# Bias rows in float32r, loads and sums tied behind other instructions, branch outputs in several DRAM tensors, and a last stage that begins by channel halves

## The chip, the cores and the metric

One Trainium2 chip, one core. The metric is the device time of one execution in microseconds (us), lower is better. The kernel before takes 1904.2 us, the median of 3 runs (1903.38 to 1905.14).

## What is computed

One step of a hybrid decoder layer: 2048 new tokens of one prompt and 8 sequences of 8 new tokens with caches, 2112 token rows in all, model width 1024, all float32. Two branches stand side by side, sliding-window attention with a learned sink and a bias by distance, and gated linear attention (GLA, 4 heads, a running state). Their outputs are projected, gated by channel, added, projected again and normalized.

```python
z = jnp.einsum('btd,dn->btn', x, w_in)
q, k, v, g_att, gq, gk, gv, g_gla, g_lr, r_att, r_gla = jnp.split(z, SPLIT_POINTS, axis=-1)
o_att = swa_prompt(...)        # s = q k / 8 + rel_bias(rel_table, dist); window of 128; softmax with a sink
new_k, new_v = ...             # samples: the cache's rows shifted by 8, then the 8 new rows
o_gla, S = gla(...)            # 4 heads, state 128 x 256 for each
h_att = jnp.einsum('bta,ad->btd', o_att * jax.nn.silu(g_att), w_pa)
h_gla = jnp.einsum('btv,vd->btd', o_gla * jax.nn.silu(g_gla), w_pg)
merged = jax.nn.sigmoid(r_att) * h_att + jax.nn.sigmoid(r_gla) * h_gla
y = jnp.einsum('btd,de->bte', merged, w_o)
x = layer_norm(DN_ALPHA * x + y, ln_g, ln_b)
```

## The kernel before

**Products.** A float32 product is made of three float32r products: each operand is split into a high part (ACT copies it, L113) and a low part (DVE, sometimes POOL, subtracts the high part, L114), and TensorE adds hi·hi, hi·lo and lo·hi in PSUM. `split` is this pair. PSUM has three banks `pd` and five banks `pa`. DVE and ACT evict the banks.

**Four stages.**
1. *Attention*, to about 365 us: six chunks of 384, 384, 384, 384, 256 and 320 tokens. For each chunk, projections k, v, four q, a narrow gl, and four gates ga, each of 8 × 3 products (`proj`, L180 to L182), whose weights come one block of 512 KB at a time (`wload`, L126). Small pieces of work, such as attention scores, wait in a list `side`: `at(d, fn)` puts one d places ahead, and `tick()`, called behind each projection, runs the first place. In chunk 0, `setup1` to `setup3` make the bias rows in this way: 8 products of 32 rows (`rb` against the one-hot `oneh`, L285) go by way of `brow` to a DRAM tensor `bs_d` and are read back shifted. At the last chunk's keys, `win` (L329 on) takes the last window of the chunk before on POOL. The shifted caches are copied straight to the outputs `o_ks` and `o_vs` by two DMAs (L418, L419).
2. *GLA*, to about 1090 us: four heads, each over the six chunks. `gla_store` writes each head's gated output to `ug_d`. `combine_x` loads two blocks of tokens, makes four sums on POOL and stores them (L839) for the stage that follows; 24 of its calls are placed here.
3. *Merge*, 1096 to 1687 us: four passes, with the weights `w_pa`, `w_ra`, `w_rg`, `w_pg`. Each does a two-by-two block product in seven products instead of eight, in the order 1, 2, 7, 6, 5, 3, 4, and each of the seven over three pairs of 352-token blocks: 84 units, numbered n, of four groups (`p`). `raw_x` loads a unit's tokens, `make_x` splits them, `raw_w` and `prep_w` do the like for weights, `partners` loads what an earlier pass left (`cs`), and `combine` evicts the bank and adds it into `a` and `fin` (L1025 to L1039). The last pass ends in `merge_sink`, which stores the merged rows to `mg_d` (L1065). Two kinds of side work are written into the loop over units: the last six `combine_x` calls, whose source is `ug_d`, at every third unit from n = 42, and `wo_load` (L1103) for the first four of eight blocks of `w_o`, at n = 64, 68, 72, 76.
4. *Last stage*, to the end: eight blocks of merged tokens are loaded and split, the other four `w_o` blocks, `lng` and `lnb` are loaded, and for each tile of 128 token rows (17 of them) both halves of 512 channels are projected (`proj_t`, 24 products each, L193 to L195; `proj_s` for the last, narrow tile). DVE adds the scaled input `xr` into `z` and gathers statistics, normalizes, and `o_y` is stored.

**Order of the work.** TensorE keeps the order of the program by hand (`manual_schedule`). The order in which every other engine, and each DMA queue, issues its instructions is fixed when the program is built, by a planner that follows the order of the program as a priority but hoists what is ready, within a pool of tiles, far ahead. A DMA is issued by an engine's queue (SP for `nc.sync`, POOL for `nc.gpsimd`), in that queue's order, and an instruction that waits holds what is behind it. Tiles of one tag are a ring of `bufs` buffers. So the sums and `w_o` loads that the program places at certain units are issued in the trace near 1203 to 1318 us, ahead of their places, and the cache copies of the last chunk at 8.44 us.

Of the kernel before, what the change touches and what calls it, by code (L numbers as in the profile page):

```python
# [21 lines left out]
P = 128  # L22
D = 1024
# [28 lines left out]
def kernel(ctx, tc, io):  # L52
# [28 lines left out]
    ua_d = dram.tile([P, 4, NT], F32, name="ua_d")  # L81
    ug_d = dram.tile([P, 8, NT], F32, name="ug_d")
    mg_d = dram.tile([P, 8, NT], F32, name="mg_d")
    ha_d = dram.tile([P, 8, NT], F32, name="ha_d")
# [27 lines left out]
    def split(dst_h, dst_l, src, eng=nc.vector):  # L112
        nc.scalar.copy(dst_h, src)  # L113
        eng.tensor_tensor(dst_l, src, dst_h.bitcast(F32), ALU.subtract)  # L114

    wseq = [0, 10]
    wready = deque()

    def wload(n=1):
        for _ in range(n):  # L120
            i = wseq[0]
            if i >= wseq[1]:
                return
            wseq[0] += 1
            st = sb.tile([P, D], F32, tag="wst", name="wst", bufs=2)
            nc.sync.dma_start(st, io["wt"][i])  # L126
# [139 lines left out]
    def setup1():  # L266

        oneh, wneg = unit(name="oneh"), unit(name="wneg")
        rtab = small([32, NH], "rtab", 1)
        nc.gpsimd.dma_start(oneh[:32, :LB], io["c_onehot"])  # L270
        nc.gpsimd.dma_start(rtab, io["rel"])
        nc.gpsimd.dma_start(wneg[:, :LB], io["c_win"].broadcast_to([P, LB]))
        nc.gpsimd.dma_start(sink, io["sink"].broadcast_to([P, NH]))
        ssel = unit(name="ssel")[:NH, :2 * P].rearrange("h (a p) -> h a p", a=2)
        scol = small([NH, 1], "scol", 1)
        nc.gpsimd.dma_start(ssel, io["c_ssel"])
        nc.gpsimd.dma_start(scol, io["sink"].rearrange("a h -> h a"))

        rb = wtile(name="rb").rearrange("p (h q) -> p h q", h=NH)[:32]
        nc.vector.tensor_copy(rb, rtab.unsqueeze(2).broadcast_to([32, NH, P]))  # L280
        for h in range(0, NH, 2):
            brow = wtile(name="brow")[:, :2 * LB].rearrange("p (h j) -> p h j", h=2)
            for j in range(2):
                bps = pa()
                mm(bps[:, :LB], rb[:, h + j], oneh[:32, :LB], start=True, stop=True)  # L285
# [28 lines left out]
    def att_keys(A, ps, T):  # L314
# [13 lines left out]
        if A["kprev"] is not None:  # L328
            kp, Tq = A["kprev"]  # L329
            win = wtile(F32R, "win").rearrange("p (a k) -> p a k", a=4)  # L330
            for i in range(4):
                nc.gpsimd.tensor_copy(win[:, i, :W], kp[i][:, Tq - W:Tq])
                nc.gpsimd.tensor_copy(win[:, i, W:], A["k"][i][:, :W])
            A["win"] = win
# [75 lines left out]
    def samp_prep(A, Tp):  # L410
# [6 lines left out]
        A["kc"], A["vc"] = kc, vc  # L417
        nc.gpsimd.dma_start(io["o_ks"][:, 0:W - TS, :], io["ck"][:, TS:W, :])  # L418
        nc.gpsimd.dma_start(io["o_vs"][:, 0:W - TS, :], io["cv"][:, TS:W, :])  # L419

# [111 lines left out]
    for c, (t0, T) in enumerate(CHUNKS):  # L532
# [45 lines left out]
        if c == 0:  # L578
            at(0, setup1)
            at(1, setup2)  # L580
            at(3, setup3)

# [40 lines left out]
        for g in range(G):  # L623
# [3 lines left out]
            if g == 1:  # L627
                xf = fetch_x(io["xT"], *CHUNKS[(c + 1) % len(CHUNKS)])
            if g == G - 2:
# [133 lines left out]
    def gla_store(B):  # L763
        for m in range(2):
            nc.sync.dma_start(ug_d[:, 2 * B["h"] + m, B["t0"]:B["t0"] + B["T"]], B["sg"][m][:, :B["T"]])

# [28 lines left out]
    def samp_b(B, bh):  # L795
# [23 lines left out]
        if bh + 4 == NB:  # L819
# [4 lines left out]
                   [(io["xT"], xc_d, 4, k, s) for s in range(MS) for k in range(4)] +  # L824
                   [(ug_d, uc_d, 4, k, s) for k0 in (0, 2) for s in range(MS) for k in (k0, k0 + 1)])

    def combine_x(new):
        src, dst, kh, k, s = combos.popleft()
        ts = slice(2 * s * MT, 2 * (s + 1) * MT)
        x1, x2 = new("x1")[:, :2 * MT], new("x2")[:, :2 * MT]  # L830
        nc.sync.dma_start(x1, src[:, k, ts])
        nc.sync.dma_start(x2, src[:, kh + k, ts])
        t0, t1 = slice(0, MT), slice(MT, 2 * MT)
# [7 lines left out]
    def chain(B):  # L841
# [10 lines left out]
        if last:  # L852
# [3 lines left out]
            at(nt + 2, lambda B=B: samp_b(B, 4))  # L856
            at(nt + 4, lambda B=B: gla_c(B, "s", NS, B["Tp"]))
            at(nt + 4, lambda B=B: gla_store(B))
        else:
# [102 lines left out]
    class Pass:  # L962
# [31 lines left out]
        def raw_x(self, i, s):  # L994
            x = mtile("xs", 4 * T, 3) if self.kh == 4 else mtile("xc", 2 * T, 5)
            if i in (1, 2, 3):
                k, t = {1: (0, 0), 2: (1, 0), 3: (1, 1)}[i]
                d = self.src[:, k * self.kh:(k + 1) * self.kh, toks(s, t)]
            else:
                d = self.kept[{7: 2, 6: 1, 5: 0, 4: 3}[i]][:, s, :self.kh]  # L1000
            nc.sync.dma_start(x.rearrange("p (k t) -> p k t", t=T), d)
            return x
# [17 lines left out]
        def combine(self, i, p, s, ps, parts):  # L1020
# [11 lines left out]
            elif i == 6:  # L1032
                a, u = acc[p, s, 12], acc[p, s, 21]
                add(a, a, ps, ALU.add)  # L1034
                nc.gpsimd.tensor_tensor(u, u, a, ALU.add)
            elif i == 5:
# [25 lines left out]
    def merge_sink(z, parts, ct, ts):  # L1062
        nc.vector.scalar_tensor_tensor(z, parts[0], 1.0, z, ALU.add, ALU.mult)
        nc.gpsimd.tensor_tensor(z, z, parts[1], ALU.add)
        nc.sync.dma_start(mg_d[:, ct, ts], z)  # L1065

    passes = [Pass(io["w_pa"], 2, ua_d, ac_d, [], store_sink),
              Pass(io["w_ra"], 4, io["xT"], xc_d, [ha_d], gated_sink),
              Pass(io["w_rg"], 4, io["xT"], xc_d, [], gate_sink),
              Pass(io["w_pg"], 4, ug_d, uc_d, [tg_d, ta_d], merge_sink)]  # L1070
    units = [(q, i, s) for q in passes for i in ORDER for s in range(MS)]
# [50 lines left out]
    for n, (q, i, s) in enumerate(units):  # L1122
        if n >= 2 * len(ORDER) * MS and n % 3 == 0 and combos:
            combine_x(lambda t: mtile("xc", 2 * T, 5))
        if n >= 3 * len(ORDER) * MS and n % 4 == 0 and len(wo) < 4:
            wo.append(wo_load(mo, len(wo), 8))
        issue_x(n + 3 if q.kh == 2 else n + 2)
# [21 lines left out]
    sb = phase.enter_context(tc.tile_pool(name="ob", bufs=1, reuse_waits="tile"))  # L1149
    x = load_x(mg_d, 0, TM)  # L1150
    for i in range(len(wo), 8):
# [4 lines left out]
    nc.sync.dma_start(lnb, io["ln_b"].broadcast_to([P, D]))  # L1156
    for t0 in range(0, NT, TM):
        for c0 in range(0, min(TM, NT - t0), P):
            n = min(P, NT - t0 - c0)
            xr = sb.tile([P, D], F32, tag="xr", name="xr", bufs=3)  # L1160
            nc.sync.dma_start(xr[:n], io["x"][t0 + c0:t0 + c0 + n])
            z = sb.tile([P, D], F32, tag="z", name="z", bufs=3)
            lastc = c0 + P >= min(TM, NT - t0)
            if lastc and t0 + TM < NT:
                xn = load_x(mg_d, t0 + TM, min(TM, NT - t0 - TM), samples=(t0 + 2 * TM >= NT))

            end = t0 + c0 + n == NT
            N = 256 if end else 512
            bst = small([P, D // 256, 6], "bst", 2)
            for i in range(D // N):  # L1170
                cs = slice(i * N, (i + 1) * N)
                ps = pd()
                wsl = slice(i * N % 512, i * N % 512 + N)
                if end:
                    rest = small([P, 256], "rest", 2)[:n, :N]
                    proj_s(ps[:, :N], rest, x, c0, wo[i * N // 512], 512, wsl)
                else:
                    proj_t(ps[:, :N], x, c0, n, wo[i * N // 512], 512, wsl)

                nc.vector.scalar_tensor_tensor(z[:n, cs], xr[:n, cs], 2.0 * ALPHA, ps[:n, :N], ALU.mult, ALU.add)  # L1180
                if end:
                    nc.vector.tensor_tensor(z[:n, cs], z[:n, cs], rest, ALU.add)
                nc.vector.bn_stats(bst[:n, i], z[:n, cs])
            mv = small([P, 2], "mv", 2)
            nc.vector.bn_aggr(mv[:n], bst[:n, :D // N].rearrange("p a s -> p (a s)"))
            rs = small([P, 1], "rs", 2)
            nc.gpsimd.tensor_scalar(rs[:n], mv[:n, 1:2], 4.0 * EPS, None, op0=ALU.add)
            nc.gpsimd.tensor_tensor(rs[:n], rs[:n], mhalf[:n], ALU.pow)
            N = 512 if end else D
            for i in range(D // N):  # L1190
# [3 lines left out]
                nc.vector.scalar_tensor_tensor(z[:n, cs], z[:n, cs], rs[:n], lnb[:n, cs], ALU.mult, ALU.add)  # L1194
                nc.sync.dma_start(io["o_y"][t0 + c0:t0 + c0 + n, cs], z[:n, cs])
        x = xn
    phase.close()
# [118 lines left out]
```

## Time and profile before

| | us |
|---|---|
| median of 3 runs | 1904.2 (1903.38 to 1905.14) |
| profiled execution | 1904.76 |
| its span | 1902.9 |
| TensorE busy | 1819.0 (96%) |
| DVE busy | 1243.9 (65%) |
| ACT busy | 847.8 (45%) |
| POOL busy | 518.2 (27%) |
| mean granted clock of TensorE | 0.983 |

The span is what the hardware profiler saw between the first and the last instruction; the profiled execution's own time has about 1.9 us beside it. A line of the timeline gives the start, the length, the engine with its source line and operation, output<-input by the program's names, shapes, and in brackets the idle time of that engine before it with what ended it. "xN" counts instructions that were joined into one line. SPq and POOL lines with DMA_DIRECT2D are the issues of DMAs, not their transfers. The granted clock is a share of TensorE's full speed: 0.50 means that a product takes twice its time. DMA share is the mean busy share of the 16 DMA engines.

### The profile page before, as it was taken

To read this page: it belongs to the slowest core of one execution; us is meant where nothing else is said; L and a number is where in the kernel's file an instruction comes from. 1 tells how busy PE (TensorE), PEld (TensorE's weight loads), DVE (VectorE), ACT (ScalarE), POOL (GpSimd) and SP (SyncE) were. 2 spreads that over 40 slices of the span, in tenths; PEclk is the share of its full clock that TensorE was granted. 3 is DMA by queue.
4 is the path that set the end of the run, shared out by engine and by line. 5 is a ranking of instruction groups with operands and counts; after the bars stand their busy time and mean duration, and the time that the engine had idled before them with its cause. 6 is when DMAs were issued, how large, how long until landed. Compare 5 with 4: busy or idle time off the path is not lost.

```text
span 1902.9 us, 32427 instructions
## 1 busy us (share of the span) xinstructions
PE 1819.0 (96%) x11683; PEld 1725.1 (91%) x11683; DVE 1243.9 (65%) x2552; ACT 847.8 (45%) x1942; POOL 518.2 (27%) x667
## 2 busy tenths in 40 slices
PE   6999999999999999999999799997999999979997
PEld 5988998889999999999999799997999999967886
DVE  4587768755675666557655559648746655956665
ACT  3444546545664664556555453434553543221100
POOL 3310111422134114213321133552322154621121
PEclk8999999999999999999999999998999999989999
DMA  6211012543365236424722289878975866884441
GB/s 223 89 38 41 25 45 86 157 144 115 106 216 179 84 122 227 146 81 147 227 79 61 78 278 309 284 268 297 322 238 169 261 216 214 272 296 168 137 138 60
DMA packets 200929, 316.03 MB, mean 166 GB/s; under 512 B 21720, under 2 KB 162864, under 8 KB 200752
## 3 DMA queue, kind: packets, MB, share of 16 engines
q1 hardware_dynamic: 195520, 307.70, 49.5%
q0 software_dynamic: 5248, 6.26, 1.2%
q8 instruction: 92, 1.51, 0.3%
q14 instruction: 69, 0.57, 0.1%
HBM read 228.72 MB, written 86.14 MB: 165 GB/s over the span
## 4 chain that ended last, share of the span: by engine, by line
PE 77%; DMA 8%; DVE 5%; POOL 4%; ACT 3%; issue 2%; SPq 1%; POOLq 0%; DVEq 0%; ACTq 0%
PE pd L180 9%; PE pd L181 9%; PE pd L182 9%; PE pa L1142 7%; PE pa L1141 7%; PE pa L1143 7%; PE pd L193 6%; PE pd L195 6%; PE pd L194 6%; PE pa L401 2%; DMA wst<-w_o 1%; DMA cs<-tg_d 1%; PE pa L386 1%; PE pa L731 1%; PE pa L732 1%
## 5 line engine op out<-in xcount | busy, mean ns | idle before, releaser
L180 PE MATMUL pd<-x,wh 128*128 128x384 f32 (+2 forms) x1248 | 409.6, 328 | 8.4 <-ACT x L113 5.3
L182 PE MATMUL pd<-x,wl 128*128 128x384 f32 (+2 forms) x1248 | 403.6, 323 | 1.3 <-DVE wl L114 1.3
L181 PE MATMUL pd<-x,wh 128*128 128x384 f32 (+2 forms) x1248 | 403.8, 324 | 0.9 <-DVE x L114 0.9
L1141 PE MATMUL pa<-xh,wh 128*128 128x352 f32 x1176 | 382.7, 325 | 17.7 <-DVE a L1034 9.7
L1142 PE MATMUL pa<-xl,wh 128*128 128x352 f32 x1176 | 380.6, 324 | 7.6 <-DVE xl L114 7.3
L1143 PE MATMUL pa<-xh,wl 128*128 128x352 f32 x1176 | 379.8, 323 | 0.0
L180 PEld LDWEIGHTS pd<-x,wh 128*128 128x128 f32 x1248 | 236.8, 190 | 17.8 <-issue 8.1
L1141 PEld LDWEIGHTS pa<-xh,wh 128*128 128x128 f32 x1176 | 222.2, 189 | 19.6 <-DVE a L1034 10.0
L181 PEld LDWEIGHTS pd<-x,wh 128*128 128x128 f32 x1248 | 236.8, 190 | 2.3 <-DVE x L114 2.1
L182 PEld LDWEIGHTS pd<-x,wl 128*128 128x128 f32 x1248 | 236.3, 189 | 1.9 <-DVE wl L114 1.9
L1142 PEld LDWEIGHTS pa<-xl,wh 128*128 128x128 f32 x1176 | 223.2, 190 | 11.9 <-DVE xl L114 11.8
L1143 PEld LDWEIGHTS pa<-xh,wl 128*128 128x128 f32 x1176 | 221.9, 189 | 0.0
L114 DVE TENSOR_TENSOR xl<-xs,xh 128x1408 fp32r<-128x1408 f32 x63 | 108.0, 1714 | 75.9 <-ACT xh L113 61.8
L113 ACT CAST x<-xst 128x384 fp32r<-128x384 f32 (+3 forms) x164 | 77.9, 485 | 160.2 <-PE pd L194 121.4
L193 PE MATMUL pd<-wh,x 128*128 128x256 f32 x512 | 148.0, 289 | 0.0
L194 PE MATMUL pd<-wh,x 128*128 128x256 f32 x512 | 144.9, 283 | 0.3 <-POOL x L114 0.2
L195 PE MATMUL pd<-wl,x 128*128 128x256 f32 x512 | 144.6, 282 | 0.0
L113 ACT CAST xh<-xs 128x1408 fp32r<-128x1408 f32 x63 | 86.4, 1372 | 99.5 <-PE pa L1143 75.4
L723 POOL TENSOR_SCALAR sq<-sq 128x1 f32<-128x1 f32 (+1 forms) x68 | 17.8, 262 | 375.3 <-ACT ring L722 375.3
L193 PE MATMUL pd<-woh,x 128*128 128x512 f32 x256 | 101.8, 398 | 13.2 <-ACT x L113 9.8
L194 PE MATMUL pd<-woh,x 128*128 128x512 f32 x256 | 101.3, 396 | 0.9 <-DVE x L114 0.9
L195 PE MATMUL pd<-wol,x 128*128 128x512 f32 x256 | 101.3, 396 | 0.6 <-DVE wol L114 0.5
(310 smaller groups left out, 3753.1 us busy)
## 6 DMA issues: line engine op xcount, KB each, us to landing
wst<-wt SPq DMA_DIRECT2D x33, 512.0 KB, 3.6
xs<-xc_d SPq DMA_DIRECT2D x24, 704.0 KB, 5.5
u<-xT SPq DMA_DIRECT2D x84, 192.0 KB, 3.9
xst<-xT SPq DMA_DIRECT2D x76, 192.0 KB, 2.7
xs<-xT SPq DMA_DIRECT2D x18, 704.0 KB, 6.1
ws<-w_ra SPq DMA_DIRECT2D x36, 256.0 KB, 4.7
ws<-w_rg SPq DMA_DIRECT2D x36, 256.0 KB, 5.1
ws<-w_pg SPq DMA_DIRECT2D x36, 256.0 KB, 3.9
```

What stands on the lines that cost most here:

```text
L113: nc.scalar.copy(dst_h, src)
L114: eng.tensor_tensor(dst_l, src, dst_h.bitcast(F32), ALU.subtract)
L180: mm(ps, hi[:, s], xh[:, :T], start=(k == 0), stop=False)
L181: mm(ps, hi[:, s], xl[:, :T], start=False, stop=False)
L182: mm(ps, lo[:, s], xh[:, :T], start=False, stop=(k == n - 1))
L193: mm(ps, xh[:, xs], hi, start=(k == 0), stop=False)
L194: mm(ps, xl[:, xs], hi, start=False, stop=False)
L195: mm(ps, xh[:, xs], lo, start=False, stop=(k == KT - 1))
L401: mm(ot[pr, :], vb[:, pr], A["pT", bi, kv][:, hf], start=(hf == h0), stop=(hf == 1))
L1141: mm(ps, wh[:, ks], xh[:, ts], start=(k == 0), stop=False)
L1142: mm(ps, wh[:, ks], xl[:, ts], start=False, stop=False)
L1143: mm(ps, wl[:, ks], xh[:, ts], start=False, stop=(k == q.kh - 1))
```

## The change

- **Start.** `setup1` makes the bias rows with two float32r products (a high and a low part of `rb`, the one-hot in float32r) in place of one in float32, and the three setup pieces run one tick later. The two cache copies are tied behind the last `win` copy, and the activation loads of chunk 1 behind the last weight load that has been written. Such a tie (`issue_after`) puts instructions of the same engine behind the named one in the issue order; it adds no wait on a semaphore.
- **DRAM tensors.** `ug_d` becomes four tensors, one for each head; `mg_d` three, one for each token pair. Loads that cross a boundary become two DMAs. In `raw_x` a block of `ug_d` is two DMAs.
- **GLA.** For heads 0 to 2 the samples' last step and store are put one place later in the list.
- **Merge.** `combine_x` is tied behind the last `raw_x` load (SP) and the last L1035 addition (POOL); `wo_load` behind the last `raw_x` load (SP) and the last high-part copy (ACT).
- **Last stage.** The rows of the loop become a class `Rows`. In the first three tiles the first half of the channels is projected for all three, and then the second half with the norm, tile by tile. `xr` and `z` have four buffers in place of three, the statistics four in place of two, and the `xr` of three tiles are loaded together.

```diff
+        pin["a"] = nc.scalar.copy(dst_h, src)
+            pin["w"] = nc.sync.dma_start(st, io["wt"][i])
...
+        oh = unit(F32R, "oh")[:32, :LB]
+        nc.scalar.copy(oh, oneh[:32, :LB])
+        rbh, rbl = (wtile(F32R, n).rearrange("p (h q) -> p h q", h=NH)[:32] for n in ("rbh", "rbl"))
+        nc.vector.tensor_copy(rbh, rt)
+        nc.vector.tensor_tensor(rbl, rt, rbh.bitcast(F32), ALU.subtract)
...
-                mm(bps[:, :LB], rb[:, h + j], oneh[:32, :LB], start=True, stop=True)
+                mm(bps[:, :LB], rbh[:, h + j], oh, start=True, stop=False)
+                mm(bps[:, :LB], rbl[:, h + j], oh, start=False, stop=True)
...
+        with tc.issue_after(pin["k"].ins):
+            nc.gpsimd.dma_start(io["o_ks"][:, 0:W - TS, :], io["ck"][:, TS:W, :])
+            nc.gpsimd.dma_start(io["o_vs"][:, 0:W - TS, :], io["cv"][:, TS:W, :])
...
-            at(0, setup1)
-            at(1, setup2)
-            at(3, setup3)
+            at(1, setup1)
+            at(2, setup2)
+            at(4, setup3)
...
+                with tc.issue_after(pin["w"].ins) if c == 0 else nullcontext():
+                    xf = fetch_x(io["xT"], *CHUNKS[(c + 1) % len(CHUNKS)])
...
+            o = nt + 4 if B["h"] == GH - 1 else nt + 5
+            at(o, lambda B=B: gla_c(B, "s", NS, B["Tp"]))
+            at(o, lambda B=B: gla_store(B))
...
+            with tc.issue_after(pin["x"].ins), tc.issue_after(pin["p"].ins):
+                combine_x(lambda t: mtile("xc", 2 * T, 5))
...
+            with tc.issue_after(pin["x"].ins), tc.issue_after(pin["a"].ins):
+                wo.append(wo_load(mo, len(wo), 8))
...
+    def load_m(t0, T, samples=False):
+        x = []
+        for k in range(KT):
+            st = xstage()
+            for s in range(t0 // (2 * MT), (t0 + T - 1) // (2 * MT) + 1):
+                a, b = max(t0, 2 * MT * s), min(t0 + T, 2 * MT * (s + 1))
+                nc.sync.dma_start(st[:, a - t0:b - t0], mg_d[s][:, k, a - 2 * MT * s:b - 2 * MT * s])
+            x.append(part((st, T), samples=samples))
+        return x
...
+    for t0 in range(0, NT, TM):
+        T = min(TM, NT - t0)
+        tiles = [Rows(x, t0, c0, T) for c0 in range(0, T, P)]
+        if t0 == 0:
+            for r in tiles:
+                r.product(0)
+        for r in tiles:
+            if r is tiles[-1] and t0 + TM < NT:
+                x = load_m(t0 + TM, min(TM, NT - t0 - TM), samples=(t0 + 2 * TM >= NT))
+            for i in range(1 if t0 == 0 else 0, D // r.N):
+                r.product(i)
+            r.norm()
```

More of the change, by code (lines that the diff above doesn't have):

```diff
@@ L2 @@
 from collections import deque
-from contextlib import ExitStack
+from contextlib import ExitStack, nullcontext
 import numpy as np
@@ L81 @@
     ua_d = dram.tile([P, 4, NT], F32, name="ua_d")
-    ug_d = dram.tile([P, 8, NT], F32, name="ug_d")
-    mg_d = dram.tile([P, 8, NT], F32, name="mg_d")
+    ug_d = [dram.tile([P, 2, NT], F32, name=f"ug{h}_d") for h in range(GH)]
+    mg_d = [dram.tile([P, 8, 2 * MT], F32, name=f"mg{s}_d") for s in range(MS)]
     ha_d = dram.tile([P, 8, NT], F32, name="ha_d")
@@ L824 @@
                    [(io["xT"], xc_d, 4, k, s) for s in range(MS) for k in range(4)] +
-                   [(ug_d, uc_d, 4, k, s) for k0 in (0, 2) for s in range(MS) for k in (k0, k0 + 1)])
+                   [(None, uc_d, 4, k, s) for k0 in (0, 2) for s in range(MS) for k in (k0, k0 + 1)])
     def combine_x(new):
@@ L830, in combine_x @@
         x1, x2 = new("x1")[:, :2 * MT], new("x2")[:, :2 * MT]
-        nc.sync.dma_start(x1, src[:, k, ts])
-        nc.sync.dma_start(x2, src[:, kh + k, ts])
+        for x_, k_ in ((x1, k), (x2, kh + k)):
+            nc.sync.dma_start(x_, ug_d[k_ // 2][:, k_ % 2, ts] if src is None else src[:, k_, ts])
         t0, t1 = slice(0, MT), slice(MT, 2 * MT)
@@ L1034, in combine @@
                 add(a, a, ps, ALU.add)
[L1035 removed]
+                pin["p"] = nc.gpsimd.tensor_tensor(u, u, a, ALU.add)
             elif i == 5:
@@ L1064, in merge_sink @@
         nc.gpsimd.tensor_tensor(z, z, parts[1], ALU.add)
-        nc.sync.dma_start(mg_d[:, ct, ts], z)
+        s = ts.start // (2 * T)
+        nc.sync.dma_start(mg_d[s][:, ct, ts.start - 2 * s * T:ts.stop - 2 * s * T], z)
     passes = [Pass(io["w_pa"], 2, ua_d, ac_d, [], store_sink),
@@ L1069 @@
               Pass(io["w_rg"], 4, io["xT"], xc_d, [], gate_sink),
-              Pass(io["w_pg"], 4, ug_d, uc_d, [tg_d, ta_d], merge_sink)]
+              Pass(io["w_pg"], 4, None, uc_d, [tg_d, ta_d], merge_sink)]
     units = [(q, i, s) for q in passes for i in ORDER for s in range(MS)]
@@ L1156 @@
     nc.sync.dma_start(lnb, io["ln_b"].broadcast_to([P, D]))
[L1157 to L1186, printed above, removed]
@@ new lines, with __init__, product, norm @@
+    class Rows:
+        def __init__(self, x, t0, c0, T):
+            self.x, self.r0, self.c0, self.n = x, t0 + c0, c0, min(P, T - c0)
+            self.end = self.r0 + self.n == NT
+            self.N = 256 if self.end else 512
+            self.xr, self.z = (sb.tile([P, D], F32, tag=n, name=n, bufs=4) for n in ("xr", "z"))
+            nc.sync.dma_start(self.xr[:self.n], io["x"][self.r0:self.r0 + self.n])
+            self.bst = small([P, D // 256, 6], "bst", 4)
+        def product(self, i):
+            n, N, xr, z, end = self.n, self.N, self.xr, self.z, self.end
+            cs = slice(i * N, (i + 1) * N)
+            ps = pd()
+            wsl = slice(i * N % 512, i * N % 512 + N)
+            if end:
+                rest = small([P, 256], "rest", 2)[:n, :N]
+                proj_s(ps[:, :N], rest, self.x, self.c0, wo[i * N // 512], 512, wsl)
+            else:
+                proj_t(ps[:, :N], self.x, self.c0, n, wo[i * N // 512], 512, wsl)
+            nc.vector.scalar_tensor_tensor(z[:n, cs], xr[:n, cs], 2.0 * ALPHA, ps[:n, :N], ALU.mult, ALU.add)
+            if end:
+                nc.vector.tensor_tensor(z[:n, cs], z[:n, cs], rest, ALU.add)
+            nc.vector.bn_stats(self.bst[:n, i], z[:n, cs])
+        def norm(self):
+            n, z = self.n, self.z
+            mv, rs = small([P, 2], "mv", 2), small([P, 1], "rs", 2)
+            nc.vector.bn_aggr(mv[:n], self.bst[:n, :D // self.N].rearrange("p a s -> p (a s)"))
```

35 lines of the change are left out of this document (15 added, 20 removed).

## The prediction

> **What bounds the kernel now.** I read the page first: its span, the busy row and the clock strip.
>
> ```profile
> span 1902.9 us, 32427 instructions
> PE 1819.0 (96%) x11683; PEld 1725.1 (91%) x11683; DVE 1243.9 (65%) x2552; ACT 847.8 (45%) x1942; POOL 518.2 (27%) x667
> PEclk8999999999999999999999999998999999989999
> ```
>
> TensorE is busy for 1819.0 of 1902.9 us, and the clock strip (40 slices, tenths of full speed) dips in three places: the 1st, the 28th and the 36th. The change leaves the float32r products as they are, so it can win only what is left: 83.9 us of idle time, and time in which TensorE is busy but at half clock. Next I read the waits of TensorE, over the span (columns: total us, times, longest) and, in the two rows after them, over the first 31 us alone.
>
> ```profile
> PE pd L193 <- ACT x L113: 9.8, 2, 9.2
> PE pa L1141 <- DVE a L1034: 9.7, 1, 9.7
> PE pa L285 <- DVE rb L280: 5.1, 1, 5.1
> ...
> PE pd L180 <- ACT wh L113: 3.1, 2, 1.9
> PE pd L182 <- DVE wl L114: 1.3, 2, 0.6
> ```
>
> The longest waits stand where the clock dips: the bias rows and first weights (start), one stall in the merge, and the entry of the last stage. Each is now taken from the timeline.
>
> **Start: the copies of the caches.** The change issues both copies (480 KB each) and the early activations of chunk 1 later.
>
> ```profile
> 8.44 0.52 POOL L418 DMA_DIRECT2D o_ks<-ck  x1
> ...
> 11.24 0.33 SPq L126 DMA_DIRECT2D wst<-wt  x1
> 11.61 1.80 SPq L145 DMA_DIRECT2D xst<-xT  x3
> 15.36 16.25 SPq L126 DMA_DIRECT2D wst<-wt  x5
> ...
> 20.32 1.04 ACT L113 CAST wh<-wst 128x1024 fp32r<-128x1024 f32 x1 [5.06 <-DMA wst<-wt]
> 21.41 0.45 PE L180 MATMUL pd<-x,wh 128*128 128x384 f32 x1 [1.94 <-ACT wh L113]
> ```
>
> The copies go out at 8.44 us, ahead of the first weights and beside them; ACT then stands 5.06 us for a weight and TensorE 1.94 us behind it. The waits for weights up to 31 us are 3.1 + 1.3 = 4.4 us. A 480 KB copy reads and writes as much as nearly two weight blocks, so its absence, with that of three activation loads on SP's queue, should bring every early weight in some microseconds sooner. I take 4.0 (bounds 1.5, if the weights are late through their own 16-engine transfer, to 4.7). Where the copies go now, behind the last window copy of chunk 5, nothing waits for them: they write outputs. The later activation loads feed chunk 1 only.
>
> **Start: bias rows.** Rows of TensorE and DVE, then three windows (columns: window, length, busy us and count of PE, PEld, DVE, ACT, POOL, then granted clock, DMA share, GB/s).
>
> ```profile
> 30.03 1.23 DVE L114 TENSOR_TENSOR wl<-wst,wh 128x1024 fp32r<-128x1024 f32 x1 [0.31 <-ACT wh L113]
> 31.18 0.67 DVE L280 COPY rb<-rtab 32x1024 f32<-32x1024 f32 x1
> 31.90 10.60 PE L285 MATMUL pa<-oneh,rb 32*128 32x384 f32 x16 [5.12 <-DVE rb L280]
> 43.08 0.69 PE L180 MATMUL pd<-x,wh 128*128 128x384 f32 x1
> ...
> 30.00:40.00 10.00, 8.10 (x13) 4.41 (x14) 4.62 (x8) 1.05 (x2) 1.12 (x2) 0.55 0.49 176
> 40.00:50.00 10.00, 10.00 (x36) 8.72 (x36) 3.04 (x6) 0.15 (x1) 5.50 (x11) 0.60 0.73 241
> 60.00:70.00 10.00, 10.00 (x60) 9.62 (x58) 5.43 (x7) 3.71 (x6) 4.66 (x12) 1.00 0.64 166
> ```
>
> Before: TensorE stops at 31.90 − 5.12 = 26.78, because `rb` is made behind a weight split on DVE and the setup needs it; 16 fp32 products follow in 10.60 us, and the next projection begins at 43.08, so 16.3 us go by. That projection (24 products) runs at about 0.60 clock: a full-clock step is 10.00/60 = 0.167 us, hence 24 × 0.167 / 0.60 = 6.7. With the value transposes of the next tick, estimated at three steps, 0.5, together 23.5.
>
> After: the setup runs one tick later, so the projection fills the hole at full clock, 24 × 0.167 = 4.0, and the 0.5 of transposes follow. The new operands `rbh`, `rbl` take their place in the ring of weight tiles one weight later, behind the next split: 31.26 + 1.23 + 0.67 + an unseen 32x1024 subtract, estimated at 0.67 to 1.8 between the copy and a 128x1024 split, or about 34.3; TensorE is free at 26.78 + 4.5 = 31.3. It waits about 3.1 (bounds 0, all ready, and 5.12, as now). Then 16 float32r products: not in the trace with 32 rows; bounds are 0.167 full clock (2.7 in all) and the 0.66 of today (10.6). I take 0.33, twice the full-clock row, since clock 0.5 will hold: 5.3, and 0.6 of sink products (43.08 − 42.50). The projection behind them pays the 2.7 of slow clock that the other paid. Sum 4.5 + 3.1 + 5.9 + 2.7 = 16.2 against 23.5, **gain 7.3** (bounds 0, with products of 0.66 and a wait of 5.12, and 15.7, with no wait, 2.7 of products and no slow clock). The one-hot copy on ACT and one more DVE instruction are below 1 us and hidden by the projection; setup2 and setup3, a tick later, feed attention a chunk on.
>
> [...] In the trace 10.6 us of unbroken 32-row products stayed at 0.55 and 0.60, and only full products lifted it, some 5 us after 43.08. [...]
>
> **Merge: the stall at 1283–1304 us.** This is where the ties on sums and output weights act.
>
> ```profile
> 1238.97 0.43 PE L1142 MATMUL pa<-xl,wh 128*128 128x352 f32 x1 [1.24 <-DVE xl L114]
> 1271.77 9.65 SPq L839 DMA_DIRECT2D uc_d<-xc  x7
> 1289.87 1.04 ACT L113 CAST woh<-wst 128x1024 fp32r<-128x1024 f32 x1 [15.44 <-DMA wst<-w_o]
> 1290.95 1.78 DVE L114 TENSOR_TENSOR wol<-wst,woh 128x1024 fp32r<-128x1024 f32 x1 [15.01 <-ACT woh L113]
> 1293.22 0.66 PE L1141 MATMUL pa<-xh,wh 128*128 128x352 f32 x1 [9.68 <-DVE a L1034]
> 1299.61 0.43 PE L1142 MATMUL pa<-xl,wh 128*128 128x352 f32 x1 [2.21 <-DVE xl L114]
> ...
> 1290.00:1295.00 5.00, 1.78 (x6) 1.78 (x7) 4.05 (x5) 4.27 (x5) 4.92 (x4) 0.50 1.00 374
> 1300.00:1305.00 5.00, 5.00 (x24) 5.00 (x23) 4.87 (x11) 3.15 (x5) 0.36 (x1) 0.66 0.91 285
> 1318.00 1.05 ACT L113 CAST woh<-wst 128x1024 fp32r<-128x1024 f32 x1 [0.77 <-DMA wst<-w_o]
> ```
>
> The output weights, written for the last pass, are hoisted far ahead: at 1289.87 ACT has stood 15.44 us for `w_o`, whose load waits on SP's queue behind stores of the sums (`uc_d`, seven issues over 9.65 us), themselves waiting for POOL. DVE stands 15.01 us behind ACT with the evictions of the product banks queued after it, and TensorE runs out of banks: 9.68, then 2.21 for a split made late, and 1.24 at 1238.97 among the same hoisted sums. At half clock (0.50 from 1293.22 to about 1297) some 1.8 us are lost, and in the other window 24 products take 5.00 us, where the row below has 19.29/121 = 0.159 us each: 1.2 more, 3.0 together. With the ties, sums issue unit by unit in the third pass, and `w_o` in the fourth, each behind the last activation load and the last split: gone are 9.68 + 2.21 + 1.24 + 3.0 = 16.1.
>
> What is late next: a tied `w_o` split on ACT waits for its own load while later splits and evictions stand behind it. The nearest row is 1318.00, a wait of 0.77, with no PE idle; four at up to 0.5 each are 2.0 (bounds 0 and 8). The fourth pass also has less room on the DMA engines:
>
> ```profile
> 1660.00:1680.00 20.00, 19.29 (x121) 18.99 (x119) 15.28 (x20) 2.75 (x2) 9.83 (x9) 1.00 1.01 341
> ```
>
> At its end the share is 1.01 and 0.71 us are lost in 20; I take as much again, 0.75, for 4 × 512 KB more in that pass. **Gain 16.1 − 2.75 = 13.4** (bounds 5, half the stall back elsewhere, to 18). The loads of `ug_d` in two pieces cost 9 more issues on SP, hidden by loads two units ahead.
>
> **Entry of the last stage.** First the order of SP's queue, then TensorE.
>
> ```profile
> 1688.31 4.86 SPq L1065 DMA_DIRECT2D mg_d<-a  x4
> 1693.22 1.87 SPq L145 DMA_DIRECT2D xst<-mg_d  x4
> 1696.84 0.80 PE L193 MATMUL pd<-woh,x 128*128 128x512 f32 x1 [9.15 <-ACT x L113]
> 1710.16 0.50 PE L193 MATMUL pd<-woh,x 128*128 128x512 f32 x1 [1.10 <-ACT woh L113]
> 1711.42 0.50 PE L195 MATMUL pd<-wol,x 128*128 128x512 f32 x1 [0.53 <-DVE wol L114]
> 1714.85 0.80 PE L193 MATMUL pd<-woh,x 128*128 128x512 f32 x1 [2.24 <-ACT woh L113]
> ...
> 1714.83 1.23 DVE L114 TENSOR_TENSOR wol<-wst,woh 128x1024 fp32r<-128x1024 f32 x1 [3.47 <-ACT woh L113]
> 1715.00:1720.00 5.00, 4.96 (x11) 3.47 (x12) 4.02 (x7) 1.00 (x2) 0.00 (x0) 0.50 0.56 206
> 1740.00:1760.00 20.00, 20.00 (x90) 16.55 (x89) 12.85 (x18) 2.03 (x4) 3.76 (x4) 1.00 0.48 166
> ```
>
> The second half of the channels needs four weights loaded only now. With three products of the first half ahead, 72 × 20.00/90 = 16 us and a little for the slow first microseconds, TensorE is busy until about 1716.5 from 1696.84; the last weight is ready at 1714.83 + 1.23 = 1716.06. So it is just covered: gone are 1.10 + 0.53 + 2.24, and the half clock of 1714.85 to about 1720.5 (5.6/2 = 2.8). **Gain 6.7** (bounds 3, if loads of `xr` ahead of the weights make these late by 4, and 8). The longer tail of z tiles is covered by a fourth buffer. The 9.15 stays: `mg_d` in three tensors lets the first tokens depend only on their own stores, but those were exact by region already, and the loads stand in SP's order behind the last stores (1688.31, then 1693.22). The straddling loads add 16 issues, spread under products. The samples' step one tick later in three heads falls to the same drain: nothing.
>
> **Sum.** 4.0 + 7.3 + 13.4 + 6.7 = 31.4. The profiled execution took 1904.76 (span 1902.9), which would come to 1873.4; the median of the runs stands 0.6 lower: 1904.2 − 31.4 = **1872.8**.
>
> **Rivals.**
> - *The split tensors free the first loads* (0.15): if SP's order changes so that the first loads pass the last stores, most of the 9.15 and the 1.7 of slow clock behind it go as well, some 10: 1862. Against it stands the queue's order above.
> - *The stall only moves* (0.18): the sums, four in turn for 9 units, still wait on POOL in the third pass and hold its loads, or `w_o` does so in the fourth; the 13.4 are lost and 18.0 stay: 1886. For it: DMA share 1.00 at the stall and 1.01 late in the fourth pass.
> - *Slower* (0.06): each of the four `w_o` loads in the fourth pass stalls ACT as at 1289.87. It decides once ACT stands longer than the five banks last, 5 × 12 × 0.159 = 9.5, as with 15.44. Then 4 × (9.68 + 2.21 + 3.0) = 60 are paid, less 16.1 + 18.0 gained: +26, about 1930. Against it: 1318.00 waited 0.77.
> - *The ties and orders do not move what issues* (0.04): the old order returns, about 1904.
>
> **How the numbers follow.** My own case has 0.57. The range 1855 to 1890 holds it with its bounds, most of the second rival's case and the first's; it leaves out the two dear cases and the ends. A measurement here can tell about 0.2% (3.8 us). Faster 0.90: my case and the first two rivals (0.57 + 0.15 + 0.18); same 0.04, where nothing moves; slower 0.06.
>
> **Right or wrong, in the changed profile.** The cache copies stand near chunk 5, and the waits for weights before 31 us are under 1 us. The bias rows are 16 float32r products near 0.33 us, behind a projection at full clock. No wait of L1034 or of its like over 2 us in the merge; `w_o` splits lie in the fourth pass; the 28th slice keeps clock 9. In the last stage the wait near 9 us remains, and none over 1 us stands before the second half. I am wrong if `w_o` or the sums show ACT or SP waits over 9 us in the passes where they land, if the bias rows wait over 5 us, or if the first load of `mg_d` comes before the last store.

## The result, and the profile after

The changed kernel takes 1880.31 us (median of 4 runs, 1876.45 to 1884.79), the kernel before 1904.67 in the same comparison (1903.38 to 1906.19). The ratio is 0.9873, with a 95% interval of 0.9849 to 0.9896: 24.4 us less, where 31.4 were forecast; the forecast time of 1872.8 was 7.5 us too low, and the range of 1855 to 1890 held the result. The profiled execution of the changed kernel took 1876.45 us, the lowest of the four, 28.3 below the profiled one of before.

The page of the changed kernel:

```profile
span 1874.7 us, 32471 instructions
PE 1812.2 (97%) x11683; PEld 1725.5 (92%) x11683; DVE 1246.1 (66%) x2553; ACT 847.6 (45%) x1943; POOL 517.2 (28%) x667
PEclk8999999999999999999999989999999999989998
```

Of its waits of TensorE (total us, times, longest), those at the places of the change and at the merge's entry:

```profile
PE pd L194 <- ACT x L113: 8.7, 2, 8.4
PE pa L1158 <- ACT wh L113: 6.9, 1, 6.9
PE pa L1159 <- DVE xl L114: 4.8, 5, 1.6
PE pa L290 <- DVE rbh L284: 4.7, 1, 4.7
```

The 9.7 us behind L1034 are gone, and so is the clock's dip in the 28th slice. The wait of the bias rows is still there, 4.7 for 5.1. A dip stands in the 24th slice (1078 to 1125 us), which the change hardly touches: it is the entry of the merge, where TensorE waits 6.9 us for `wh` and the granted clock is 0.53 from 1086 to 1092 us and 0.62 from there to 1098. The kernel before waits 7.2 there and has 0.54 from 1092 to 1098, at the border of two slices, so that its strip does not show it.

The two timelines by stage, in us: the first gate of chunk 0 is evicted at 58.13 (before 65.48), the last gate of the GLA stage at 1076.11 (1079.97), the merge's first product starts at 1091.74 (1095.87), the last stage's at 1676.33 (1696.84), and the span ends at 1874.7 (1902.9). So the lead is 7.4 behind the start, only 3.9 at the end of the GLA stage, 4.1 at the merge, 20.5 at the last stage and 28.2 at the end.

*The start.* The changed kernel's timeline, DVE and TensorE:

```profile
29.38 1.22 DVE L114 TENSOR_TENSOR wl<-wst,wh 128x1024 fp32r<-128x1024 f32 x1 [1.92 <-ACT wh L113]
30.63 0.55 DVE L349 SCALAR_TENSOR_TENSOR qa<-pd,qa 64x384 fp32r<-64x384 f32 x1
31.20 0.56 DVE L350 SCALAR_TENSOR_TENSOR qb<-pd,qb 64x384 fp32r<-64x384 f32 x1
31.79 0.56 DVE L581 COPY vt<-pa 128x384 f32<-128x384 f32 x1
32.38 0.68 DVE L284 CAST rbh<-rtab 32x1024 fp32r<-32x1024 f32 x1
...
33.21 0.66 PE L290 MATMUL pa<-oh,rbh 32*128 32x384 f32 x1 [4.70 <-DVE rbh L284]
40.10 0.69 PE L181 MATMUL pd<-x,wh 128*128 128x384 f32 x1
```

Two of its windows, columns as in the prediction:

```profile
34.00:40.00 6.00, 5.64 (x19) 5.64 (x19) 4.65 (x9) 1.04 (x1) 0.65 (x2) 0.50 0.40 147
40.00:45.00 5.00, 5.00 (x16) 4.99 (x17) 2.63 (x5) 0.00 (x0) 2.80 (x6) 0.50 1.00 281
```

The projection does fill the old hole, but `rbh` is not made beside it. It stands on DVE behind the next weight split (29.38 to 30.60, as the prediction had it) and then behind that projection's own evictions (`qa`, `qb`, `vt`, 1.7 us together), which run only after TensorE is done at 28.51. The 16 products go at 0.32 us as forecast (19 in 6.00 us with the sink products), at a granted clock of 0.50, and the projection behind them begins at 0.50 too.

*The merge.* The changed kernel's timeline, one of the tied sums in the third pass and one of the tied output weights in the fourth:

```profile
1355.81 0.95 POOL L842 TENSOR_TENSOR xc<-xc 128x352 f32<-128x352 f32 x1 [2.54 <-DMA xc<-ug_d]
...
1561.24 0.42 SPq L1120 DMA_DIRECT2D wst<-w_o  x1
1567.56 1.05 ACT L113 CAST woh<-wst 128x1024 fp32r<-128x1024 f32 x1 [8.43 <-DMA wst<-w_o]
```

Both stand where they were tied. ACT waits 8.43 us for `w_o`, much more than the 0.77 I had taken, and still TensorE has no wait over 1.6 us in the merge behind its first product: the banks cover it.

*The last stage.* The changed kernel's timeline, SP's queue and TensorE's first product:

```profile
1668.53 4.53 SPq L1080 DMA_DIRECT2D mg_d<-a  x4
1673.11 1.87 SPq L1174 DMA_DIRECT2D xst<-mg_d  x4
1676.33 0.80 PE L194 MATMUL pd<-woh,x 128*128 128x512 f32 x1 [8.41 <-ACT x L113]
```

Then the split of the last of the four weights that the second half needs, and the window in which the products of the second half begin (the first at 1696.42):

```profile
1693.93 1.23 DVE L114 TENSOR_TENSOR wol<-wst,woh 128x1024 fp32r<-128x1024 f32 x1 [2.80 <-ACT woh L113]
...
1696.33:1702.33 6.00, 6.00 (x29) 4.95 (x28) 3.82 (x8) 0.93 (x2) 0.00 (x0) 1.00 0.65 200
```

The first loads of merged rows stand behind the last stores, as before. The waits for `woh` and `wol` are gone: the last weight is ready at 1695.16, 1.3 us before its first use, and TensorE is busy in every microsecond of 1696 to 1702.

### The profile page after: what moved, and what is told of

Same layout as the page of the kernel before. It is cut to its first block, busy times and chain, and to the rows that moved or that the text cites. A ratio compares the mean times of both kernels' runs of the same rounds, so it can differ in the third digit from the quotient of the medians.

```text
span 1874.7 us, 32471 instructions
## 1 busy us (share of the span) xinstructions
PE 1812.2 (97%) x11683; PEld 1725.5 (92%) x11683; DVE 1246.1 (66%) x2553; ACT 847.6 (45%) x1943; POOL 517.2 (28%) x667
## 4 chain that ended last, share of the span: by engine, by line
PE 80%; DMA 6%; DVE 5%; POOL 3%; ACT 3%; issue 2%; SPq 1%; POOLq 0%; DVEq 0%; ACTq 0%
PE pd L181 9%; PE pd L182 9%; PE pd L183 9%; PE pa L1159 8%; PE pa L1158 8%; PE pa L1160 8%; PE pd L195 6%; PE pd L196 6%; PE pd L194 6%; PE pa L407 2%; PE pa L392 1%; PE pa L739 1%; PE pa L740 1%; PE pa L738 1%; DMA cs<-tg_d 1%
## 5 line engine op out<-in xcount | busy, mean ns | idle before, releaser
L181 PEld LDWEIGHTS pd<-x,wh 128*128 128x128 f32 x1248 | 237.2, 190 | 15.6 <-issue 8.1
L114 DVE TENSOR_TENSOR xl<-xs,xh 128x1408 fp32r<-128x1408 f32 x63 | 111.9, 1776 | 74.5 <-ACT xh L113 55.6
L195 PEld LDWEIGHTS pd<-wh,x 128*128 128x128 f32 x512 | 98.4, 192 | 2.4 <-DVE x L114 2.4
```

The costliest lines, as they stand in the source:

```text
L181: mm(ps, hi[:, s], xh[:, :T], start=(k == 0), stop=False)
L195: mm(ps, xl[:, xs], hi, start=False, stop=False)
```

## The experiments

My theory after the two traces: the parts add, and start, merge and last stage bring 7.4, 15.6 and 7.7 us in the profiled executions (between the merge's first product and the last stage's the lead grows by 16.4; 0.7 of it is the shorter wait at the last stage's entry). What was open: why the first gate's lead was 7.4 and not 11.3, what took 3.5 us of it back before 1080 us, and why the median stands 4 us above the profiled execution. Times below are medians, each beside the kernel before on the same chip, with the ratio's 95% interval.

**The changed kernel again.** No edit.

> The changed kernel unaltered. Its first four runs spread over 8.3 us (1876.45 to 1884.79), the kernel before over 2.8. Theory: the spread comes from the output weights in the fourth pass, where ACT stood 8.43 us for w_o at 1567.56 and the five banks last about 9.5; then a slower profiled run shows TensorE waiting some us behind a w_o split there, and the other stages as in the first profile. Rival: it comes from the start or the GLA stage (clock at half after short idle times, some 1.5 us each); then the fourth pass looks as in the first profile and the loss stands before 1095 us. Both expect 1876 to 1885.

1877.75 against 1905.22, ratio 0.9856 (0.9837 to 0.9876). In its profile (1877.12, not one of the longer executions) the fourth pass has no wait of TensorE over 1.6 us. In the GLA stage the clock held at 1067 us, but fell at another place: the granted clock is 0.57 from 723 to 727 us. And the kernel before, 17 runs here, spread from 1899.08 to 1908.13 by itself. So the spread that I wished to explain belongs to no part of the change: the first theory fell, and of the rival only the clock (below) is shown.

**The start alone.** The diff's part for `setup1`, the ticks, the cache copies and `fetch_x`, on the kernel before.

> The kernel before with the start's part alone: bias rows in float32r, setup one tick later, both cache copies tied late, activation loads of chunk 1 tied. Theory (the parts add, and the start brought 7.4 us by the first gate and 5.4 by the end of the GLA stage): 1897 to 1900, spread under 4 us, TensorE waiting over 4 us for rbh. Rival (the loss of 2.0 us near 319 us and the half clock near 1067 us belong to other parts of the change): 1897 with the full 7.4 kept to 1090 us.

1895.58 against 1905.22, ratio 0.9952 (0.9936 to 0.9967): 9.6 us less, somewhat more than either theory; the spread, 1893.19 to 1902.67, is more than the 4 of the theory. First gate at 57.49, wait for `rbh` 4.17. Its lead of 8.0 there has shrunk to 2.5 where the merge starts (1093.35 for 1095.87): 2.0 are lost near 319 us as in the changed kernel, and the clock falls at 1066 us here too. So these losses are no matter of the other parts, and the rival fell. But this was the longest of six executions, and the other five took 1897.39 or less: the rest of the loss is not the kernel's for certain.

**The merge alone.**

```diff
+            with tc.issue_after(pin["x"].ins), tc.issue_after(pin["p"].ins):
+                combine_x(lambda t: mtile("xc", 2 * T, 5))
...
+            with tc.issue_after(pin["x"].ins), tc.issue_after(pin["a"].ins):
+                wo.append(wo_load(mo, len(wo), 8))
```

> The kernel before with the ties of the sums and of wo_load alone. Theory (this part took 15.6 us out of the merge in the profile, and carries the spread): 1889 to 1897, spread over 4 us, a wait of ACT for w_o of 5 to 12 us in the fourth pass. Rival (the stall moves with time as soon as a transfer is late): 1900 or more. The other rival (spread from elsewhere): 1889 to 1890 with a spread under 3 us.

1889.35, ratio 0.9917 (0.9900 to 0.9935): 15.9 us less, as the profiles had it. The spread was 7.9, and ACT's longest wait for `w_o` in the fourth pass 7.67, both as the theory had them.

**The last stage alone.** `Rows` with `load_x` from one `mg_d`.

> The kernel before with the last stage by channel halves alone (four buffers of xr and z), merged rows in one tensor as before. Theory: the wait for the other four weights goes, 7.7 us, and the entry's wait near 9 us stays: 1896 to 1898, spread under 3 us. Rival (the DRAM split is needed for the entry): the wait of the entry is longer than the 8.4 us of the changed kernel by more than 0.7, and 1897 to 1900.

1902.20, ratio 0.9989 (0.9977 to 1.0002): 3.0 us less, not 7.7, and the interval takes in no change at all; the spread was 11.1. The entry's wait was 8.16. The theory had the right waits and the wrong worth. Compare the first product of the last stage to the end: 200.5 us here, 198.4 in the changed kernel, 206.1 in the profile of before; but the six other kernels of this document whose last stage is that of before have 201.5 to 205.9. The window just behind the wait for the last weight in the kernel before (granted clock: third column from the end):

```profile
1716.84:1722.84 6.00, 6.00 (x20) 4.73 (x19) 4.60 (x7) 1.00 (x2) 1.97 (x2) 0.69 0.41 136
```

And in the kernel with the start alone:

```profile
1717.39:1723.39 6.00, 6.00 (x28) 4.96 (x27) 5.43 (x9) 0.97 (x2) 1.98 (x2) 1.00 0.44 143
```

The same work, 20 products against 28 in 6 us: the profiled execution of before had lost its clock there, and the other had not. What I had counted as the kernel's is partly the execution's. Of the seven profiles with the old last stage, before and the loads alone had 6.8 us of half clock behind those weights, the merge alone and its two parts 3.4, the start alone and the bias rows alone none; TensorE waited 0.3 to 4.1 us for the four weights. Over the seven the stage took 204.3 us in the mean, and over the seven profiles with the new one 199.2 (198.3 to 201.4): about 5 us, between the 3.0 of the times and the 7.7 of the first pair.

**Parts of the start.** First the copies and the loads of chunk 1 alone, then the float32r rows alone, at the old tick.

> The kernel before with the cache copies and the activation loads of chunk 1 tied late, nothing else. Theory (the early weights shared the DMA engines with the copies): the waits for weights up to 31 us fall from 4.4 to about 1.2 us, the first gate of chunk 0 comes 2.5 to 3.5 us earlier than at 65.48, the time 1901 to 1903. Rival (the weights are late through their own transfers): 4 us of waits remain, 1905.

The waits of TensorE before 31 us, in this kernel:

```profile
PE pa L286 <- DVE rb L281: 4.1, 1, 4.1
PE pd L183 <- DVE wl L114: 0.4, 1, 0.4
```

4.4 us of waits for weights became 0.4, and the first gate came at 60.87, 4.6 earlier. The mechanism is shown; the time, 1903.25 against 1904.35, ratio 0.9990 (0.9975 to 1.0005), does not stand clear of no change. The loads of chunk 1 and the cache copies were moved together here; which of them held up the weights was not tried. In chunk 5 a wait appears that the kernel before does not have there:

```profile
321.81 1.07 PE L402 MATMUL pa<-pT,vt 128*64 128x512 f32 x2 [1.13 <-DVE pT L389]
```

The lead falls there from 4.6 to 2.6 us.

> The kernel before with the float32r bias rows alone, the setup at its old tick. Theory (the later tick brought nothing, since the new wait for rbh, 4.0 to 4.7 us behind the evictions of the next projection on DVE, stands for the old one of 4.1 to 5.1): 16 products at 0.32 us after a wait near 5 us, first gate 4.5 to 5.5 us earlier, the time 1899 to 1901, and this with loads_only makes the 9.6 of the start. Rival (the later tick is worth the projection in the hole, 2 to 3 us, as predicted): first gate only 2 to 3 us earlier, 1902 to 1903.

The first of the float32r products in its timeline:

```profile
33.21 0.66 PE L289 MATMUL pa<-oh,rbh 32*128 32x384 f32 x1 [5.32 <-DVE rbh L283]
```

And the window over the products:

```profile
34.00:40.00 6.00, 5.64 (x19) 5.64 (x19) 4.65 (x9) 0.08 (x1) 0.33 (x1) 0.50 0.59 215
```

First gate at 62.99, 2.5 earlier than before's; 1900.31, ratio 0.9973 (0.9960 to 0.9985). The gate's lead is the rival's, the time the theory's. By the gates, 4.6 and 2.5 of the 7.4 to 9.0 (five profiles with the whole start) are these two, and the later tick is left with 0.3 to 1.9 us. But the first gate comes at 64.14 to 67.43 in the five profiles with the old start, so what the tick is worth stays open between the theory's nothing and the rival's 2 to 3.

**Parts of the merge.** The sums' tie alone, and the `w_o` tie alone.

> The kernel before with the ties of combine_x alone; the w_o loads keep their old hoisted places. Theory (w_o was late because it stood behind the stores of the sums on SP): the wait of 9.7 us goes, as w_o no longer stands behind them, 1889 to 1892. Rival (the hoisted w_o loads stall ACT anyway, by DMA share 1.00): a wait over 5 us stays near 1290 us, 1897 to 1901.

1892.48, ratio 0.9933 (0.9916 to 0.9951): 11.9 us less. In this kernel TensorE's waits between 1200 and 1330 us are short, nearly all for splits:

```profile
PE pa L1144 <- DVE xl L114: 2.9, 3, 1.2
PE pa L1143 <- ACT xh L113: 0.6, 1, 0.6
PE pa L1143 <- DVE fin L1029: 0.3, 1, 0.3
```

The `w_o` loads still come early here, but no longer behind the sums' stores, and ACT waits 3.9 us for them at most.

> The kernel before with the ties of wo_load alone; the six sums stay hoisted near 1203 to 1300 us. Theory (the stall needs both: ACT in order behind a late w_o): the 9.7 goes here as well, and a smaller loss of 1 to 4 us stays where SP stands behind the sums, 1890 to 1895. Rival (SP standing behind the sums delays the units' own loads): over 5 us stay near 1290 us, 1897 to 1901.

1898.86, ratio 0.9961 (0.9947 to 0.9976): 5.5 us less. The 7.9 us that stay have another last link. TensorE's wait in this kernel between 1200 and 1330 us:

```profile
PE pa L1143 <- DVE a L1040: 7.9, 1, 7.9
```

And its timeline, SP's queue and DVE:

```profile
1274.77 10.83 SPq L840 DMA_DIRECT2D uc_d<-xc  x7
1300.18 0.64 SPq L1057 DMA_DIRECT2D ta_d<-fin  x1
1306.48 0.52 DVE L1039 TENSOR_TENSOR fin<-a,pa 128x352 f32<-128x352 f32 x1 [8.47 <-DMA ta_d<-fin]
```

SP stands behind the stores of the sums, so the stores of finished rows (`ta_d`) come late, their `fin` buffers are not free, and DVE, with nothing to do with `w_o`, holds the banks. The cause is the hoisted sums on SP's queue; `w_o` was only the first to suffer. The rival was right here.

**The operands one tick earlier.** On the changed kernel, `setup1` in two:

```diff
+        st1["ops"] = oh, rbh, rbl, wneg, ssel, scol
+
+    def setup1b():
+        oh, rbh, rbl, wneg, ssel, scol = st1["ops"]
...
-            at(1, setup1)
+            at(0, setup1)
+            at(1, setup1b)
```

> The changed kernel with setup1 in two: the operands oh, rbh, rbl and the small loads one tick earlier (place 0), the products at place 1 as in the change. Theory (the wait of 4.0 to 4.7 us for rbh is only its place on DVE behind the evictions of the next projection): no wait over 1 us for rbh, first gate 4.5 us or more earlier than 57.2 to 58.1, so 51 to 53; if without the idle time the clock stays full through the 16 rows and the next projection, another 4 to 5. Time 1868 to 1874. Rival (rbh is late because rtab, oneh or a tile comes late): the wait stays over 3 us, 1877 to 1880.

Its timeline, DVE and TensorE:

```profile
27.17 0.68 DVE L284 CAST rbh<-rtab 32x1024 fp32r<-32x1024 f32 x1
31.41 0.56 DVE L585 COPY vt<-pa 128x384 f32<-128x384 f32 x1
...
32.03 0.68 PE L294 MATMUL pa<-oh,rbh 32*128 32x384 f32 x1 [1.40 <-DVE vt L585]
```

And its windows:

```profile
28.00:32.00 4.00, 2.16 (x11) 1.42 (x9) 3.90 (x5) 2.50 (x4) 0.00 (x0) 0.87 0.60 179
32.00:36.00 4.00, 3.97 (x13) 3.87 (x14) 4.00 (x10) 1.04 (x1) 0.00 (x0) 0.50 0.73 270
```

`rbh` is ready at 27.85 and the products begin at 28.24 with no wait; first gate at 53.80, 3.4 to 4.3 earlier than with the change, a little less than the theory's 4.5. After eight products the banks are full, since DVE still has `qa`, `qb` and `vt` ahead of the first `brow`: a wait of 1.40, and the clock falls after all. The products before it, at full clock, follow each other every 0.17 us, those behind it every 0.32. 1874.36 against 1903.90, ratio 0.9835 (0.9813 to 0.9858): the lowest ratio of all, though its interval overlaps that of the changed kernel. The wait for `rbh` was its place on DVE, as the theory had it; the further 4 to 5 us of clock did not come.

**The output weights' splits two units later.** On the changed kernel, the load at n = 64, 68, 72, 76, its split tied at n + 2; then with the edit above.

> The changed kernel with the split of each of the four early w_o blocks tied two units behind its load. Theory (the wait of ACT of 8.43 us was covered by the five banks): no wait of ACT for w_o over 1 us in the fourth pass, and the time the same within 2 us, 1876 to 1880. Rival (this wait is what costs the 1 to 1.6 us behind each split, DVE's xl): 3 to 5 us less, 1873 to 1875.

1879.31 against 1903.90, ratio 0.9869 (0.9846 to 0.9891); ACT's wait for `w_o` is gone in the fourth pass, and TensorE's wait for a split of 1.6 there is 2.15. So the 8.43 us had cost nothing that these times can tell, as the theory had it, and the spread (1875.83 to 1883.44) stayed as well.

> rb_early and wo_late together. Theory: as rb_early within 2 us, 1868 to 1874. Rival of wo_late: 3 to 5 us below rb_early.

1875.26, ratio 0.9845 (0.9822 to 0.9868), within 1 us of the operands alone and 1.3 above the theory's range.

**The DRAM tensors in one piece.** `ug_d` and `mg_d` undivided and the samples' step at its old place, all else as in the change.

> The changed kernel with ug_d and mg_d as one tensor each, and the samples' step at its old place. Theory (dependencies were exact by region, the first load of the last stage stands behind the last store in SP's order): the wait at the entry stays 8 to 9 us, the time the same within 2 us as the changed kernel, 1876 to 1881. Rival (the split frees the first loads by some tenths): entry 0.5 us or more longer, and 1880 or more.

SP's queue and TensorE's first product of the last stage in this kernel:

```profile
1668.13 4.68 SPq L1073 DMA_DIRECT2D mg_d<-a  x4
1672.86 1.87 SPq L146 DMA_DIRECT2D xst<-mg_d  x4
1676.03 0.79 PE L194 MATMUL pd<-woh,x 128*128 128x512 f32 x1 [8.45 <-ACT x L113]
```

The same order, and 8.45 for 8.41 us. 1881.73, the median of four executions (a fifth took 5079.22 us, for a reason that nothing here shows, and is left out), ratio 0.9877 (0.9854 to 0.9900): not to be told from 0.9869 and 0.9873. The median lies 0.7 us above the range that the theory gave. In the profile the last stage took 201.4 us for 198.4: TensorE waited 1.07 and 0.88 for `x` (0.29 and 0.88 in the changed kernel), and the granted clock fell to half for 3.4 us behind them. Whether the single tensor or the execution made that wait longer was not tried.

## Why the prediction was right, and where it was off

- **Sign and size.** Start, merge and last stage alone gave 9.6, 15.9 and 3.0 us, 28.5 together; all of them on the same chip 27.5 (1905.22 to 1877.75), and 24.4 in the first comparison. Forecast were 11.3, 13.4 and 6.7, so the merge came out larger and the other two smaller. That the sum came so near owes something to luck: its errors have opposite signs.
- **Early weights (4.0).** Right in mechanism: 4.4 us of waits fell to 0.4 in the kernel with the loads alone. In the changed kernel's profile 0.51 and 0.64 were left (1.15, a little over the 1 us forecast) and the first product came 0.38 later, so the projection ahead of the old hole ended 2.8 earlier (33.21 − 4.70, less 4.5 for the next projection and the transposes, is 24.0, against 26.78).
- **Bias rows (7.3): the term that was mis-sized.** The step that failed is the wait of 3.1. I placed `rbh` directly behind the next weight split; between the two stand 1.7 us of evictions of the very projection that was to hide it, so 4.70 and, for `rbl`, 0.50 were paid. Both operands were ready at 34.30, the forecast's 34.3; but TensorE was free at 28.51 and not at 31.3, since the earlier weights had brought it forward and the operands had not come forward with it. The two terms of the start were added as if they had. This 5.2 is at the edge of the sign that the prediction gave for being wrong, over 5 us. The working becomes 4.5 + 5.2 + 6.4 + 2.6 = 18.7 for 16.2, a gain of 4.8 for 7.3. Width and rate of the products (0.32 for 0.33) and the slow clock behind them (2.6 for 2.7: 24 products from 40.10 to 46.74, less 4.0) were right. The 2.8 above and this 4.8 make 7.6, and the first gate's lead was 7.4. With the operands a tick earlier the first gate came another 3.4 to 4.3 us sooner.
- **What was not in the sum.** Behind the start the lead fell from 7.4 to 3.9 in the changed kernel's profile: 2.0 in chunk 5, where DVE's order differs (`kl` now behind the softmax's `es`, a wait of 1.13 for `pT` that the kernel before does not have there), and 1.6 by the clock at 1067 us. The kernel with the loads alone has the same order, the same wait of 1.13 and the same loss; the one with the bias rows alone keeps its 2.6. So the 2.0 come with the copies and loads that were moved, which the prediction put at nothing (nothing waits for them): 2.0 of the 4.6 us that they win at the start are paid back in chunk 5. That the DVE order costs it was read, not tried. The 1.6 belong to the execution: the second profile of the changed kernel kept its clock there and lost 1.7 at 723 us, and the merge alone, whose code is as before up to 1095 us, loses 3.5 on the same way.
- **Merge (13.4).** The stall went as forecast; 15.6 and 15.9 were measured: the new costs of 2.75 that I had set aside do not show. In seven profiles with both ties the merge takes 585.0 us in the mean, in five with neither 601.6. The rival of the moved stall and the slower one, which turned on ACT waiting longer than the banks last (9.5), came near with 8.43 but did not decide. My chain had `w_o` as the needed link; the two halves showed that the sums on SP's queue are, worth 11.9 alone against 5.5.
- **Last stage (6.7).** The cover by three products of the first half held, and the waits are gone. Mis-sized by the half clock, and that by chance: the profile of before has 6.8 us of it there, priced at 2.8, where five of the seven old profiles have 3.4 or none. The times give 3.0 (4.4 less to 0.4 more), the lengths of the stage about 5.
- **DRAM tensors and the samples' step (0).** Right: same order, same wait at the entry, and a time that the spread does not tell apart. The rival that the first loads pass the last stores did not come.

## What to carry to other kernels

SP's queue, blocked here by stores that waited on POOL, starved what stood behind it, and tying the sums alone won 11.9 us; look for what is hoisted onto a queue before blaming the engine that waits. When an operand is to be hidden behind a product, check its place in its own engine's order: behind that product's evictions, 1.7 us here, `rbh` was not early, and TensorE waited 4.70 us for it. A load that is moved out of the way need not be free at its new place (of the 4.6 us won here, 2.0 were lost again in chunk 5): look there too. And before a half-clock stretch of one profile enters a sum, as the 6.8 us of the last stage did, look for it in several executions.

## What the runs showed of the hardware

The clock after the same short idle time differs between executions. Windows around a wait of 2.30 us in the GLA stage, in the kernel before:

```profile
1067.00:1072.00 5.00, 2.70 (x21) 2.46 (x20) 2.77 (x9) 1.55 (x5) 1.38 (x3) 1.00 0.04 13
1072.00:1075.00 3.00, 3.00 (x24) 2.77 (x23) 1.00 (x4) 0.91 (x3) 0.00 (x0) 1.00 0.49 129
```

The same place in the changed kernel:

```profile
1062.00:1067.00 5.00, 2.70 (x17) 2.46 (x17) 2.36 (x8) 1.54 (x5) 1.38 (x3) 0.88 0.09 28
1067.00:1070.00 3.00, 3.00 (x16) 3.00 (x16) 0.79 (x3) 0.47 (x2) 0.00 (x0) 0.62 0.49 107
```

TensorE is busy for 2.70 of 5.00 us in both; one goes on at 1.00, the other at 0.62, and loses 1.6 us.

Behind the wait, from 1065.9 to 1069.0 us, the 128x320 products of the changed kernel follow each other every 0.27 us, those of the kernel before every 0.15. The granted clock fell behind this wait in one profile and not in the other; why is not shown.

The products of 32 rows ran for 6 us at 0.50 in the changed kernel, in float32r, as they had for 10.60 us at 0.50 in float32 in the kernel before, and the clock came back only about 5 us after full products began (40.10, then 45.06; before, 43.08, then 48.05).

Single runs of the kernel before spread from 1897.37 to 1910.66 us in 26 runs on one chip, against 1.8 us in the three runs that the prediction had.
